# The first gate/up pair of an FFN: from a classical product to three seven-product units whose first two products run ahead

## The chip, the cores and the metric

The kernel runs on one core of one Trainium2 chip. The metric is the device time of one execution in microseconds (us), lower is better. It is called "same" below when the two kernels differ by less than 0.2%, which is about 4 us here.

PE is TensorE's matrix multiplication and PEld its weight load, DVE is VectorE, ACT is ScalarE, POOL is GpSimd, SP is the engine that issues most DMAs.

## What is computed

A decoder trunk of two layers over 512 tokens of width 1024, everything in float32. Each layer has two feed-forward blocks (FFNs), a mixer and a cross-attention, each behind an RMS norm, so there are four FFNs in the program:

```python
def swiglu_ffn(h, w_gu, w_down):
    gu = h @ w_gu                                  # 1024 -> 2 x 2816
    gate, up = jnp.split(gu, 2, axis=-1)
    return (jax.nn.silu(gate) * up) @ w_down       # 2816 -> 1024
...
x = x + 0.5 * rms_norm(swiglu_ffn(rms_norm(x, g_pre), w_gu, w_down), g_post)
```

## The kernel before

Every float32 product is made of three matmuls on rounded parts. `split` (L73) writes the rounded part `hi` of a tensor with a ScalarE copy (a cast, L74) and the remainder `lo` with a VectorE subtraction (L75); `mm3` (L77 to L81) then issues hi*hi, hi*lo and lo*hi into one PSUM bank. Weights are split in the same way after their DMA (`whi`, `wlo` in the profile).

**The norm in front of an FFN.** The 512 tokens are four tiles of 128. For each, `rms_transpose` (L160) takes the mean square (ACT L166, DVE L168 and L171), the reciprocal root on GpSimd (L158), and the scaled copy on ACT (L175). Its inner function `turn` transposes that tile on PE (L182, eight 128x128 blocks), multiplies by the gain on VectorE (L184) into the raw quarters, and splits the result. The first two tiles are turned before the FFN starts, the third and fourth inside it.

**An FFN** (`ffn`, L557) has 22 blocks of 128 hidden units, taken as 11 gate/up pairs `j` = 0, 2, ... 20 in three parts (0 to 8, 8 to 16, 16 to 22). Behind each of the first two parts comes the down-projection `seven_tm` (L336), whose matmuls are 128x512; behind the last comes `tm_last`.

**Ten of the pairs** go through `seven` (L292): a 2x2 block product by seven multiplications in place of eight. Its operands are the four quarters of the normalised activations (a11 and a12 are the first token half, a21 and a22 the second), and four combinations of them, x1 to x4, that `Quarters.ready` (L137) makes once for each FFN, after the fourth tile is turned. Each product is 24 matmuls of 128x256, so a pair has 7 x 24 = 168. Products p1 and p2 use a11 and a12, the first token half alone. The five others use x2, x1, x3, x4 and a22, and need all four tiles. Two weight sums, t1 and t3, are made by a DMA that adds on landing, issued on GpSimd's queue (L297, L302).

**The first pair, j = 0,** goes through `fm_quad` (L276), the classical product: four blocks of 24 matmuls over the first token half, then four over the second, 192 in all. `TURNS` puts the turns of tile 3 and tile 4 behind the first and the third block of the first half in the code 

```python
for c0 in (0, HALF):
    for i, (w, p_) in enumerate(zip(ws, ps)):
        fm_mm(p_, w, a, KD, c0, c0 + HALF)
        if c0 == 0 and i in TURNS:
            pre.turn()
```

Its weights are loaded and split early by `Prenorm.warm`. The order of each queue follows the code, a scheduler that moves instructions a little, and tile pools (PSUM pool `pa` for the banks `psa`, SBUF pool for `big`, `q4`, `raw`).

## Time and profile before

| | before |
|---|---|
| median of 3 runs | 2004.55 us (2003.13 to 2005.48) |
| the profiled execution | 2006.68 us, span 2005.0 us |
| PE busy | 1951.0 us, 97% of the span |
| DVE busy | 1488.6 us, 74% |
| ACT busy | 1038.3 us, 52% |
| POOL busy | 233.8 us, 12% |

The profiled execution is 2.1 us longer than the median; its span lacks 1.7 us of its own time. In rows of a timeline the first number is the start in us of the span, then the busy time, engine, line, operation, out<-in, shape and the number of instructions. What stands in brackets is the engine's idle time before it and what ended it. Matmuls of one row overlap; the time that one costs is the distance between starts.

### The profile page before, as it was taken

Reading aid. Unit: us, or ns where it says so; the run is one execution under the profiler, and the core shown is the slowest. Engines: PE = TensorE matmul, PEld = TensorE weight load, DVE = VectorE, ACT = ScalarE, POOL = GpSimd, SP = SyncE. Lnnn points to the kernel's source line nnn. Section 1 sums busy time; section 2 is a strip of 40 time slices with the busy share of each in tenths; the row PEclk is TensorE's granted clock in tenths of the full one; section 3 lists DMA queues with packets and bytes.
Section 4 is the critical chain, followed back from the end, with each engine's and each line's share of the span. In section 5 each row is a group of like instructions: output and inputs, shape, how many; then the busy total and the mean of one; then the engine's idle time right before and its main releaser. Section 6 shows DMA issues by size and latency. Waiting matters only on the chain.

```text
span 2005.0 us, 31807 instructions
## 1 busy us (share of the span) xinstructions
PE 1951.0 (97%) x12841; PEld 1784.3 (89%) x12841; DVE 1488.6 (74%) x1831; ACT 1038.3 (52%) x1477; POOL 233.8 (12%) x229
## 2 busy tenths in 40 slices
PE   7999999998998999999999999999999999999998
PEld 7989899887878889899898989999878889999897
DVE  6787877799956458877877887787666648776974
ACT  6555555543555455545555555555545545555552
POOL 1111110122001011111101111110000001111100
PEclk9999999999999999999999999999999999999999
DMA  7887884323642145887972788886152225898871
GB/s 201 219 213 185 204 207 140 118 85 126 224 154 95 53 107 142 208 204 187 221 213 65 172 217 179 202 212 185 63 179 74 85 53 138 209 211 200 202 187 42
DMA packets 250281, 319.90 MB, mean 160 GB/s; under 512 B 9756, under 2 KB 189556, under 8 KB 249110
## 3 DMA queue, kind: packets, MB, share of 16 engines
q1 hardware_dynamic: 193510, 242.32, 38.3%
q0 software_dynamic: 56448, 75.51, 21.9%
q8 instruction: 100, 1.64, 0.3%
q14 instruction: 47, 0.39, 0.1%
q10 hardware_dynamic: 176, 0.05, 0.0%
HBM read 311.54 MB, written 6.29 MB: 159 GB/s over the span
## 4 chain that ended last, share of the span: by engine, by line
PE 80%; DVE 8%; issue 5%; ACT 3%; POOL 2%; DMA 1%; POOLq 0%; ACTq 0%; SPq 0%; DVEq 0%
PE psa L81 26%; PE psa L80 26%; PE psa L79 26%; DVE wlo L75 2%; POOL r L158 1%; DVE big L75 1%; DVE big L730 1%; ACT q L175 1%; ACT whi L74 1%; PE tps L182 1%; DMA raw<-in_ffn_w_gu_dram 1%; ACT q L166 1%; DVE h L479 0%; DVE raw L404 0%; DVE q L394 0%
## 5 line engine op out<-in xcount | busy, mean ns | idle before, releaser
L81 PE MATMUL psa<-big,wlo 128*128 128x256 f32 (+1 forms) x3056 | 885.2, 290 | 6.6 <-DVE wlo L75 6.6
L79 PE MATMUL psa<-big,whi 128*128 128x256 f32 (+1 forms) x3056 | 884.4, 291 | 6.5 <-ACT big L74 4.6
L80 PE MATMUL psa<-big,whi 128*128 128x256 f32 (+1 forms) x3056 | 887.1, 291 | 0.8 <-DVE big L75 0.8
L74 ACT CAST whi<-raw 128x1024 fp32r<-128x1024 f32 x522 | 546.2, 1050 | 601.5 <-PE psa L80 263.1
L75 DVE TENSOR_TENSOR wlo<-raw,whi 128x1024 fp32r<-128x1024 f32 x522 | 636.0, 1225 | 252.8 <-ACT whi L74 250.1
L79 PEld LDWEIGHTS psa<-big,whi 128*128 128x128 f32 x3056 | 586.8, 193 | 17.1 <-ACT big L74 8.5
L81 PEld LDWEIGHTS psa<-big,wlo 128*128 128x128 f32 x3056 | 587.6, 193 | 15.0 <-DVE wlo L75 7.8
L80 PEld LDWEIGHTS psa<-big,whi 128*128 128x128 f32 x3056 | 588.3, 193 | 9.2 <-DVE big L75 1.8
L79 PE MATMUL psa<-whi,big 128*128 128x512 f32 x864 | 339.3, 393 | 7.7 <-ACT big L74 6.2
L80 PE MATMUL psa<-wlo,big 128*128 128x512 f32 x864 | 336.9, 390 | 0.0
L81 PE MATMUL psa<-whi,big 128*128 128x512 f32 x864 | 336.1, 392 | 0.4
L79 PEld LDWEIGHTS psa<-whi,big 128*128 128x128 f32 x864 | 162.4, 188 | 44.3 <-ACT big L74 10.3
L81 PEld LDWEIGHTS psa<-whi,big 128*128 128x128 f32 x864 | 162.2, 188 | 39.3 <-DVE big L75 5.8
L80 PEld LDWEIGHTS psa<-wlo,big 128*128 128x128 f32 x864 | 162.3, 188 | 33.1 <-DVE wlo L75 0.6
L302 POOL DMA_DIRECT2D raw<-in_ffn_w_gu_dram x40 | 51.6, 1289 | 582.1 <-DMA raw<-in_ffn_w_gu_dram 360.0
L158 POOL TENSOR_TENSOR r<-m,nhalf 128x1 f32<-128x1 f32 x74 | 49.0, 662 | 463.5 <-DVE m L533 181.7
L297 POOL DMA_DIRECT2D raw<-in_ffn_w_gu_dram x40 | 52.6, 1316 | 314.2 <-DMA raw<-in_ffn_w_gu_dram 236.3
L352 POOL DMA_DIRECT2D raw<-in_ffn_w_down_dram x48 | 57.4, 1227 | 261.9 <-DMA raw<-in_ffn_w_down_dram 187.0
L730 DVE SCALAR_TENSOR_TENSOR big<-big,par 128x511 f32<-128x511 f32 (+29 forms) x120 | 85.7, 770 | 0.0
L79 PE MATMUL psa<-big 128*128 128x512 f32 (+1 forms) x224 | 80.9, 363 | 0.8 <-ACT big L74 0.8
L80 PE MATMUL psa<-big 128*128 128x512 f32 (+1 forms) x224 | 80.7, 360 | 0.0
L81 PE MATMUL psa<-big 128*128 128x512 f32 (+1 forms) x224 | 80.2, 359 | 0.0
(150 smaller groups left out, 1658.6 us busy)
## 6 DMA issues: line engine op xcount, KB each, us to landing
raw<-in_ffn_w_gu_dram SPq DMA_DIRECT2D x216, 512.0 KB, 4.7
raw<-in_ffn_w_down_dram SPq DMA_DIRECT2D x120, 512.0 KB, 4.2
raw<-in_ffn_w_gu_dram POOLq DMA_DIRECT2D x80, 512.0 KB, 7.9
raw<-in_ffn_w_down_dram POOLq DMA_DIRECT2D x48, 512.0 KB, 7.8
raw<-in_xa_w_kv_dram SPq DMA_DIRECT2D x32, 512.0 KB, 3.5
raw<-in_ev_w_in_dram SPq DMA_DIRECT2D x16, 512.0 KB, 4.3
raw<-in_xa_w_q_dram SPq DMA_DIRECT2D x16, 512.0 KB, 4.4
raw<-in_xa_w_o_dram SPq DMA_DIRECT2D x16, 512.0 KB, 3.5
```

Source lines behind the costliest of these rows:

```text
L74: nc.scalar.copy(out=hi, in_=src)
L75: nc.vector.tensor_tensor(out=lo, in0=src, in1=hi.bitcast(F32), op=ALU.subtract)
L79: nc.tensor.matmul(out=ps, lhsT=lhs[0], rhs=rhs[0], start=start, stop=skip, skip_group_check=skip)
L80: nc.tensor.matmul(out=ps, lhsT=lhs[0], rhs=rhs[1], start=False, stop=skip, skip_group_check=skip)
L81: nc.tensor.matmul(out=ps, lhsT=lhs[1], rhs=rhs[0], start=False, stop=stop or skip, skip_group_check=skip)
L158: nc.gpsimd.tensor_tensor(out=r, in0=m, in1=nhalf.broadcast_to([P, n]), op=ALU.pow)
L166: nc.scalar.activation(out=xn[:, hs[i]], in_=src[:, hs[i]], func=AF.Square, accum_out=ss[i])
L175: nc.scalar.activation(out=xn[:, hs[i]], in_=src[:, hs[i]], func=AF.Copy, scale=r)
L297: nc.gpsimd.dma_start(out=t1, in_=fm_rows(w, 0, ca), accum_op=ALU.add)
L302: nc.gpsimd.dma_start(out=t3, in_=fm_rows(w, 1, cb), accum_op=ALU.add)
L352: nc.gpsimd.dma_start(out=raws[kk], in_=rows(kh, kk, ch), accum_op=ALU.add)
L730: nc.vector.scalar_tensor_tensor(out=acc[:, c, s_:], in0=z[:, c, :SEQ - s_], scalar=par[:, c, CONV - 1 - s_:CONV - s_], in1=acc[:, c, s_:] ...
```

## The change

The classical pair goes. All 11 pairs of an FFN run through `seven`, which becomes a generator that stops behind p1 and p2. The first three pairs (`AHEAD` = 3) do their p1 and p2 one after the other, with the turn of tile 3 behind the first unit's and that of tile 4 behind the second's; then each is run to its end. The first two units' p1 and p2 weights are the ones that `warm` prepares (columns 0 and 256 of the gate half in place of gate and up). `ready` works in place and makes x2 first, then x1, x3 and x4; the split of a21, which the classical pair alone used, is dropped.

```diff
+AHEAD = 3
...
+        def operand(src):
+            o = ops4()
+            split(o[:, 0], o[:, 1], src)
+            return o
...
             def block(self, i, c0, c1):
+                if c0 >= HALF and i == 0:
+                    return None
...
             def ready(self):
                 r0, r1 = self.raws
                 a11, a12, a21, a22 = r0[:, :, :HALF], r1[:, :, :HALF], r0[:, :, HALF:], r1[:, :, HALF:]
-                sub, add = ALU.subtract, ALU.add
-                xs = [ops4() for _ in range(4)]
-                e = qt([P, 4, HALF])
-                for i, (p_, q_, op) in enumerate(((a21, a22, sub), (e, a11, sub), (a12, e, add), (a11, a21, sub))):
-                    if i == 3:
-                        e = qt([P, 4, HALF])
-                    nc.vector.tensor_tensor(out=e, in0=p_, in1=q_, op=op)
-                    split(xs[i][:, 0], xs[i][:, 1], e)
-                self.x1, self.x2, self.x4, self.x3 = xs
+                sub = ALU.subtract
+                tt = nc.vector.tensor_tensor
+                tt(out=a11, in0=a11, in1=a21, op=sub)
+                tt(out=a21, in0=a21, in1=a22, op=sub)
+                nc.vector.scalar_tensor_tensor(out=a22, in0=a11, scalar=-1.0, in1=a22, op0=ALU.mult, op1=sub)
+                self.x2, self.x1, self.x3 = operand(a22), operand(a21), operand(a11)
+                tt(out=a12, in0=a12, in1=a22, op=ALU.add)
+                self.x4 = operand(a12)
...
-                    hi, lo = x.block(i, c0, c1)
-                    split(hi, lo, raw)
+                    to = x.block(i, c0, c1)
+                    if to:
+                        split(*to, raw)
...
-        def seven(w, ca, cb, x, done, mid=None):
-            t1 = fm_raw(w, 0, cb)
-            nc.gpsimd.dma_start(out=t1, in_=fm_rows(w, 0, ca), accum_op=ALU.add)
-            b11 = fm_raw(w, 0, ca)
-            b21 = fm_raw(w, 1, ca)
-            b22 = fm_raw(w, 1, cb)
-            t3 = fm_raw(w, 0, cb)
-            nc.gpsimd.dma_start(out=t3, in_=fm_rows(w, 1, cb), accum_op=ALU.add)
-            banks = {n: psa().rearrange("p (u n) -> p u n", u=2) for n in "ABC"}
+        def seven(w, ca, cb, x, done, mid=None, ahead=None):
+            later = ahead is not None
+            def sum_t1():
+                t1 = fm_raw(w, 0, cb)
+                nc.gpsimd.dma_start(out=t1, in_=fm_rows(w, 0, ca), accum_op=ALU.add)
+                return t1
+            if not later:
+                t1 = sum_t1()
+            b11, b21 = (None, None) if ahead else [fm_raw(w, i, ca) for i in range(2)]
+            def rest():
+                b22 = fm_raw(w, 1, cb)
+                t3 = fm_raw(w, 0, cb)
+                nc.gpsimd.dma_start(out=t3, in_=fm_rows(w, 1, cb), accum_op=ALU.add)
+                return b22, t3
+            if not later:
+                b22, t3 = rest()
+            banks = {n: psa().rearrange("p (u n) -> p u n", u=2) for n in "AB"}
             out_a = qt([P, 2, SEQ])
-            out_b = qt([P, 2, SEQ])
...
-            p1 = product("A", b11, x.a11, True)
+            wh = ahead or (None, None)
+            p1 = product("A", b11, x.at(0, 0), True, wh[0])
             nc.scalar.copy(out=out_a[:, :, lo_h], in_=p1)
-            p2 = product("B", b21, x.a12, True)
+            p2 = product("B", b21, x.at(0, 1), True, wh[1])
             nc.vector.tensor_tensor(out=out_a[:, :, lo_h], in0=p2, in1=out_a[:, :, lo_h], op=add)
+            yield
+            if later:
+                t1 = sum_t1()
+                b22, t3 = rest()
+                b11 = raw_tile([P, 4, 256])
+                b21 = fm_raw(w, 1, ca)
+            out_b = qt([P, 2, SEQ])
+            banks["C"] = psa().rearrange("p (u n) -> p u n", u=2)
...
                 for j in range(j0, j1, 2):
                     to = None if ending else r[(j - j0) // 4][:, (j - j0) % 4:(j - j0) % 4 + 2, :]
-                    if j == 0:
-                        ws = pre.ws
-                        ps = fm_quad([ws[0], ws[2], ws[1], ws[3]], pre, True)
...
-                        continue
...
-                    seven(w_gu, j * P, FF + j * P, pre.x, done, mid)
-                    if not ending and j - j0 == 2:
-                        a11 = ops4()
-                        split(a11[:, 0], a11[:, 1], r[0][:, :, :HALF])
+                    ahead = ([*pre.ws, ()][j // 2]) if j // 2 < AHEAD else None
+                    unit = seven(w_gu, j * P, FF + j * P, pre.x, done, mid, ahead)
+                    next(unit)
+                    if j // 2 < AHEAD:
+                        units.append(unit)
+                        if j // 2 < AHEAD - 1:
+                            pre.turn()
+                            continue
+                        for unit in units[:-1]:
+                            list(unit)
+                            prepare()
+                        unit = units[-1]
+                    list(unit)
+                    prepare()
...
-            return Prenorm(col(n, l), w[l], (0, FF), True)
+            return Prenorm(col(n, l), w[l], (0, 256), True)
```

PE's queue in the second FFN, before: the fourth tile's transposes (`tps`) stand in the fourth block of the first half (`psa_7156` is a bank of the classical pair, `psa_7418` to `psa_7420` those of pair 2; `big_7264` is x2, `big_7263` is x1).

```order
L81 MATMUL psa_7156<-big_7051,wlo_7120 128x256
...
L182 MATMUL tps_7255<-ident_85,q4_7138 128x128 x4
L79 MATMUL psa_7156<-big_7060,whi_7123 128x256
...
L79 MATMUL psa_7155<-big_7187,whi_7107 128x256
...
L79 MATMUL psa_7418<-big_7051,whi_7423 128x256
...
L79 MATMUL psa_7419<-big_7060,whi_7452 128x256
...
L79 MATMUL psa_7418<-big_7264,whi_7482 128x256
```

There are 156 matmuls between the second group of transposes and the first that reads x2. And now (`psa_7310`, `psa_7311` are the third unit's banks, `psa_7155` the first unit's, `big_7293` is x2, `big_7296` is x1):

```order
L184 MATMUL tps_7276<-ident_85,q4_7140 128x128 x4
L184 MATMUL tps_7282<-ident_85,q4_7140 128x128 x4
L80 MATMUL psa_7310<-big_7053,whi_7313 128x256
...
L82 MATMUL psa_7311<-big_7062,wlo_7343 128x256
L80 MATMUL psa_7155<-big_7293,whi_7385 128x256
L80 MATMUL psa_7383<-big_7296,whi_7414 128x256
L81 MATMUL psa_7155<-big_7293,whi_7385 128x256
```

48 matmuls are left between them, the third unit's p1 and p2, and one matmul of x1's product stands inside the first of x2's.

VectorE's queue at the same place, from the fourth tile's multiplies to x2's remainder, before:

```order
L184 TENSOR_TENSOR big_6720<-tps_7247,cols_101 128x4x128
L184 TENSOR_TENSOR big_6721<-tps_7255,cols_101 128x4x128
L75 TENSOR_TENSOR big_7187<-big_6720,big_7187 128x4x128
L146 TENSOR_TENSOR q4_7267<-big_6720,big_6721 128x1024
L75 TENSOR_TENSOR big_7196<-big_6721,big_7196 128x4x128
L146 TENSOR_TENSOR q4_7277<-big_6720 128x1024
L75 TENSOR_TENSOR big_7263<-q4_7267,big_7263 128x1024
L146 TENSOR_TENSOR q4_7267<-q4_7267,big_6720 128x1024
L75 TENSOR_TENSOR big_7264<-q4_7267,big_7264 128x1024
```

And now, with the three instructions that stand ahead of the multiplies:

```order
L76 TENSOR_TENSOR wlo_7343<-raw_7308,whi_7342 128x1024
L351 TENSOR_TENSOR raw_7379<-raw_7371,raw_7374 128x1024
L342 TENSOR_TENSOR q4_7225<-psa_7224,q4_7225 128x2x256
L186 TENSOR_TENSOR big_6722<-tps_7276,cols_101 128x4x128
L186 TENSOR_TENSOR big_6723<-tps_7282,cols_101 128x4x128
L145 TENSOR_TENSOR big_6722<-big_6722 128x4x256
L76 TENSOR_TENSOR big_7220<-big_6723,big_7220 128x4x128
L146 TENSOR_TENSOR big_6722<-big_6722,big_6723 128x4x256
L76 TENSOR_TENSOR wlo_7386<-raw_7379,whi_7385 128x1024
L147 SCALAR_TENSOR_TENSOR big_6723<-big_6722,big_6723 128x4x256
L342 TENSOR_TENSOR q4_7312<-psa_7311,q4_7312 128x2x256
L149 TENSOR_TENSOR big_6723<-big_6723 128x4x256
```

Behind the last row comes x2's remainder (L76). A weight remainder, a weight sum and an output sum now stand ahead of the multiplies, and a weight remainder and an output sum among the steps that lead to x2.

GpSimd's queue in the third FFN, before (`r1_10518` and `r1_10530` are square roots of the third tile's norms):

```order
L158 TENSOR_TENSOR r1_10518<-m_10515,nhalf_90 128x1
L297 DMA raw_11118<-in_ffn1_w_gu_dram 128x4x256
L158 TENSOR_TENSOR r1_10530<-m_10528,nhalf_90 128x1
```

And now:

```order
L160 TENSOR_TENSOR r1_10522<-m_10519,nhalf_90 128x1
L160 TENSOR_TENSOR r1_10534<-m_10532,nhalf_90 128x1
```

The accumulating DMA no longer stands between the two.

## Rows read from the trace of the kernel before

**Rows 1.** The page: busy time, share of the span and instructions of each engine:

```profile
PE 1951.0 (97%) x12841; PEld 1784.3 (89%) x12841; DVE 1488.6 (74%) x1831; ACT 1038.3 (52%) x1477; POOL 233.8 (12%) x229
```

**Rows 2.** The page: shares, by engine, of the chain that ended last:

```profile
PE 80%; DVE 8%; issue 5%; ACT 3%; POOL 2%; DMA 1%; POOLq 0%; ACTq 0%; SPq 0%; DVEq 0%
```

**Rows 3.** Timeline of PE: first 128x512 product of each FFN (start, us busy, engine, line):

```profile
104.08 0.40 PE L79 MATMUL psa<-whi,big 128*128 128x512 f32 x1
...
825.79 0.40 PE L79 MATMUL psa<-whi,big 128*128 128x512 f32 x1
...
1167.82 0.40 PE L79 MATMUL psa<-whi,big 128*128 128x512 f32 x1
...
1743.08 0.40 PE L79 MATMUL psa<-whi,big 128*128 128x512 f32 x1
```

**Rows 4.** Timeline of PE: gate/up matmuls, first and second FFN:

```profile
17.57 0.42 PE L81 MATMUL psa<-big,wlo 128*128 128x256 f32 x1
...
21.63 0.34 PE L80 MATMUL psa<-big,whi 128*128 128x256 f32 x1
...
752.02 0.28 PE L79 MATMUL psa<-big,whi 128*128 128x256 f32 x1
752.14 0.28 PE L80 MATMUL psa<-big,whi 128*128 128x256 f32 x1
```

**Rows 5.** Timeline of PE: tile-4 transposes of the second to fourth FFN, tile 3's of the third:

```profile
750.56 0.66 PE L182 MATMUL tps<-ident,q 128*128 128x128 f32 x4 [1.89 <-ACT q L175]
...
1082.93 0.66 PE L182 MATMUL tps<-ident,q 128*128 128x128 f32 x4
...
1091.92 1.27 PE L182 MATMUL tps<-ident,q 128*128 128x128 f32 x8 [0.17 <-ACT q L175]
...
1667.85 0.66 PE L182 MATMUL tps<-ident,q 128*128 128x128 f32 x4 [2.33 <-ACT q L175]
```

**Rows 6.** Timeline of DVE, second FFN: before the tile-4 multiplies, and from them:

```profile
748.87 0.16 DVE L171 SCALAR_TENSOR_TENSOR m<-ss,m 128x1 f32<-128x1 f32 x1
751.25 1.30 DVE L184 TENSOR_TENSOR big<-tps,cols 128x512 f32<-128x512 f32 x2 [2.23 <-PE tps L182]
...
753.24 1.22 DVE L146 TENSOR_TENSOR q<-big 128x1024 f32<-128x1024 f32 x1
754.38 0.68 DVE L75 TENSOR_TENSOR big<-big 128x512 fp32r<-128x512 f32 x1
754.98 1.22 DVE L146 TENSOR_TENSOR q<-big 128x1024 f32<-128x1024 f32 x1
```

**Rows 7.** Timeline of ACT, second FFN: the last norm output; a table load for Silu:

```profile
749.78 1.33 ACT L175 ACTIVATE q<-h,r 128x512 f32<-128x512 f32 x2 [0.95 <-POOL r L158]
...
755.56 1.28 ACT L571 ACT_TABLE_LOAD   x1
```

**Rows 8.** Timeline of POOL, second and third FFN: accumulating DMAs and square roots:

```profile
744.71 1.32 POOL L302 DMA_DIRECT2D raw<-in_ffn_w_gu_dram  x1 [7.94 <-ACT big L74]
745.55 1.08 POOL L158 TENSOR_TENSOR r<-m,nhalf 128x1 f32<-128x1 f32 x1
...
1080.22 1.31 POOL L297 DMA_DIRECT2D raw<-in_ffn_w_gu_dram  x1 [5.14 <-DVE m L171]
1081.04 1.08 POOL L158 TENSOR_TENSOR r<-m,nhalf 128x1 f32<-128x1 f32 x1
```

**Rows 9.** Timeline of PE: a long wait elsewhere in the program:

```profile
458.66 0.58 PE L81 MATMUL psa<-big,wlo 128*128 128x256 f32 x1 [2.76 <-DVE wlo L75]
```

**Rows 10.** Windows (range, length, PE, PEld, DVE, ACT, POOL, PEclk, DMA share, GB/s):

```profile
460.00:464.00 4.00, 4.00 (x28) 4.00 (x28) 4.00 (x7) 1.03 (x1) 0.00 (x0) 0.74 0.35 124
...
752.00:756.00 4.00, 4.00 (x34) 3.90 (x33) 3.93 (x5) 2.70 (x4) 0.00 (x0) 1.00 0.63 101
...
736.00:832.00 96.00, 92.39 (x738) 89.91 (x736) 76.40 (x84) 52.95 (x68) 11.84 (x11) 1.00 0.66 168
```

**Rows 11.** The page: accumulating DMAs of the gate/up weights, us to landing:

```profile
raw<-in_ffn_w_gu_dram POOLq DMA_DIRECT2D x80, 512.0 KB, 7.9
```

33 lines of the change are left out of this document (15 added, 18 removed).

## The prediction

> **What bounds the kernel now.** I read the page first. PE is busy for 97% of the span [rows 1], and the chain that ended last runs on PE for 80% of the span [rows 2], so time is won by fewer matmuls and lost by any wait of PE. VectorE at 74% is the next engine, busy enough to be late in a burst. Then I read PE's timeline at the four FFN entries, since only these four places change. At the low clock a 128x256 matmul costs 4.06 / 19 = 0.213 us (19 matmuls between the first two rows), at the high one 0.12 [rows 4]. The four marks that I compare are the starts of the first 128x512 product, that of the first down-projection: 104.08, 825.79, 1167.82 and 1743.08 [rows 3]. Up to the mark the program changes; behind it the queues are as before.
>
> **The change, part by part.**
>
> *Removed:* the classical pair has 192 matmuls and the seven-product one 168. That is 24 less for each FFN, or 24 x 0.12 = 2.9 us, and 11.5 us over four. This lies on PE and counts in full as long as PE does not wait.
>
> *Added beside the matmuls:* 24 more VectorE and 16 more ScalarE instructions, and 24 more weight DMAs (12.6 MB of 320 MB). Over the second FFN's first part ScalarE is busy 53 of 96 us and the DMA engines have a share of 0.66 [rows 10], so I cost these at nothing there. VectorE with 76 of 96 us has less room; what it has to do at the entry is the next part. If its cover went, each of its 24 instructions would cost at most 1.14 us (below), 27 us in all; I take nothing except where I count them one by one.
>
> *Moved:* this is where the gain goes. `ready` can start only when tile 4 is transposed, and PE then needs matmuls that do not use x2. Before, 156 of them stand there, 18.7 us. Now 48, the third unit's p1 and p2: 48 x 0.12 = 5.8 us. Against it stands VectorE's queue from the first multiply of tile 4 to x2's remainder, as the new order has it: two multiplies and two short instructions (a22's remainder and an output sum) at 0.60, from 754.38 to 754.98, and six long ones at 1.14, from 753.24 to 754.38 [rows 6]: the three in-place sums, the `scalar_tensor_tensor` among them, that the trace of before does not show (I take it as a two-input sum of the same size; between 0.60 and 2 x 1.14 it could be 0.5 less or 1.1 more), a weight remainder, the sum for x4 and x2's remainder. Together 4 x 0.60 + 6 x 1.14 = 9.2, say 9.3 us with the hand-over between engines. So PE waits even if VectorE starts at once: transposes start, first multiply 0.69 later [rows 5, 6], 9.3 more, less 1.15 for the transposes and 5.8 for the cover: 3.0 us. That the third unit's sums also stand ahead of the first multiply makes it longer:
>
> - Second FFN. The fourth tile's scaled norm starts at 749.78 and PE takes it up at 750.56 after 1.89 idle [rows 5, 7]. The copy of an output sum and its neighbours now stand ahead on ScalarE, so I start the transposes 0.55 later, at 751.1, and end them at 752.3. VectorE is through with the last mean at 749.0 [rows 6], has a weight remainder and a weight sum (1.14 each) and two output sums (0.6) in front, so it comes to the multiply at 752.6, 1.5 after the transposes began. x2 is ready at 752.6 + 9.3 = 761.9. PE's cover ends at 752.3 + 5.8 = 758.1: a wait of 3.9 us, cut by two lone matmuls that need only the rounded parts of x2 and x1. From x2 to the mark there are 526 matmuls, 63.1 us.
> - The clock. After a wait of 2.76 us [rows 9] the granted clock is 0.74 of full in the window behind it, while after the 1.89 us at 750.56 it is 1.00 [rows 5, 10]. Our wait is nearer to the first, so I charge some 20 matmuls at the low cadence, 20 x (0.213 - 0.12) = 1.9 us; the bounds are nothing and twice that.
> - So the mark comes at 761.9 + 63.1 + 1.9 = 826.9: **+1.1** against 825.79. The fourth FFN has the same distance from transposes to mark before (75.23 us in both, [rows 3, 5]): **+1.1** too.
> - Third FFN. Now the accumulating DMA (1.31 us) does not stand between tile 3's square roots on GpSimd [rows 8], so tile 3's transposes start about 1.3 earlier than 1082.93 [rows 5], at 1081.6. With 1.1 for them and 95 matmuls (11.4) tile 4's start at 1094.1; before, at 1091.92, since fewer matmuls stood ahead. First multiply 1.5 later as above, x2 at 1104.9, mark at 1169.9: **+2.1** against 1167.82.
> - First FFN. At 21.63, when the clock rises [rows 4], 22 of the 96 matmuls of the first two units are done; 74 x 0.12 and 1.1 for tile 3's transposes set tile 4's to 31.6. A Silu table load of 1.28 [rows 7] now stands on ScalarE ahead of tile 3's last cast, on which VectorE's next remainder waits, so the first multiply is 2.8 later, at 34.4; x2 at 43.7, mark at 108.7: **+4.6** against 104.08.
>
> Sum: 4.6 + 1.1 + 2.1 + 1.1 = +8.9 us. The profiled execution (2006.68) lies 2.1 above the median of the runs, 2004.55; the differences carry over, so I predict 2004.55 + 8.9 = **2013.5**.
>
> **The rivals.**
>
> *The clock holds.* If the wait costs no clock, 1.9 goes at each entry. In the second and fourth FFN the next wait then shows: the weight remainder of x1's product stands in VectorE's queue behind the other operands' remainders, four of 1.14 = 4.6 us behind x2's, against 2.9 us of x2's own matmuls, so 1.7 come back. The sum is 2.7 + 0.9 + 0.2 + 0.9 = +4.7, 2009.2. For it: the waits of 1.89 and 2.33 us at tile 4 of before [rows 5], the first followed by a clock of 1.00 [rows 10]. Against it: PE does hardly anything for 4 us. The Trainium skill, "TensorE: Matmul & The Clock Gate", section "Why this matters for your kernels", advises to leave no long idle gaps between bursts of matmuls, or the engine falls back; as the two lone matmuls cut the gap in pieces, the rule would speak for this rival. The wait in rows 9 agrees with the rule; no row of before shows a cut gap.
>
> *Late weight sums.* Units 2 and 3 each need t1 and t3, two accumulating DMAs for each 120 matmuls (14.4 us) where before it was two for each 168 (20.2 us), and they are issued only when the first unit has begun to finish. Each takes 7.9 us to land [rows 11] behind a load of the same tile. If they come 1 us late for each of the two units, each entry costs 2 us more: +16.9, 2021.5. For it: GpSimd is idle much of the time, but its DMA waits for what was loaded. Against it: the DMA share of 0.66 [rows 10] leaves room.
>
> *The stall is small (the other side).* If VectorE meets the first multiply as the transposes land, in place of 1.5 to 2.8 us later, and the clock holds, x2 comes 0.69 + 9.3 after the transposes. The price of the wait then is 3.0 us against 2.9 saved. GpSimd decides it: before, the square root of the last tile stood behind an accumulating DMA of 1.32 [rows 8], which now is issued later, so that the last tile can be normalised and transposed earlier and VectorE has its other work behind it. With the transposes at 750.2 in the second FFN x2 is ready at 760.2 and the mark at 823.3, -2.5, likewise in the fourth; third 1094.1 + 10.0 + 63.1 = 1167.2, -0.6; first 31.6 + 10.0 + 63.1 = 104.7, +0.6. Sum -5.0, 1999.5. The point from which it decides is the first multiply of tile 4 starting within 0.7 us of the first transpose. Against it: the new order puts a weight remainder and a weight sum in front of the multiply on the same engine, 2.3 us of work.
>
> That the change does not do what it says can be left out: the new order shows 168 matmuls and 48 of cover.
>
> **How the numbers follow.** Forecast 0.5; clock holds 0.2; late sums 0.15; small stall 0.1; 0.05 for anything beyond. About 0.2% (4 us) is what a measurement can tell from no change, so "same" reaches from 2000.5 to 2008.6. The clock's rival lies at its edge and takes half of its chance there, and the forecast's lower part a tenth: same 0.18. Small stall and a little more: faster 0.09. The rest is slower: 0.73. The range leaves out the small stall and what lies beyond late sums: 2003 to 2022, which also takes in the clock's double price (4 x 1.9 = 7.6 more than 2013.5).
>
> **What would show it.** In the profile of the changed kernel: 96 matmuls of 128x256 less; at each entry PE's idle of 3 to 5 us in front of the first matmuls with x2, put down to VectorE's `big` (its remainder) or ScalarE's cast; a granted clock below 1 in the 4 us behind it; VectorE's first multiply of tile 4 at least 1.5 us behind the first transpose; the marks 1 to 5 us later. It is wrong if the clock stays at 1.00 behind the wait, if the wait is under 2 us, or if PE waits for a DMA (`raw`) or a weight remainder in the units that finish.

## The result and the profile after

The changed kernel takes 2023.47 us (median of 4 runs, 2022.49 to 2025.78) where the kernel before takes 2005.01 on the same chip: a ratio of 1.0093, with a 95% interval of 1.0081 to 1.0106. That is slower, as forecast, but by 18.5 us and not by 8.9; it lies above the range of 2003 to 2022. The profiled executions differ by 15.8 us in their spans (2005.0 and 2020.8); the one of before lies 1.7 above its median, the one of after 1.0 below, which makes the 18.5.

The page of after, to be read against [rows 1, 2]:

```profile
PE 1949.8 (96%) x12745; PEld 1781.1 (88%) x12745; DVE 1512.2 (75%) x1855; ACT 1050.0 (52%) x1493; POOL 245.6 (12%) x237
...
PE 75%; DVE 10%; issue 5%; ACT 4%; POOL 2%; DMA 2%; POOLq 0%; ACTq 0%; SPq 0%; DVEq 0%
```

The 96 matmuls are gone, yet PE is busy 1.2 us less only (a matmul at the low clock, below, is busy 0.41 us in place of 0.28), and PE's share of the chain fell from 80% to 75%: 2 points went to VectorE, one each to ScalarE and the DMAs. The four marks (timeline of PE, first 128x512 product of each FFN, as in [rows 3]):

```profile
109.81 0.40 PE L80 MATMUL psa<-whi,big 128*128 128x512 f32 x1
...
834.96 0.40 PE L80 MATMUL psa<-whi,big 128*128 128x512 f32 x1
...
1178.27 0.40 PE L80 MATMUL psa<-whi,big 128*128 128x512 f32 x1
...
1758.87 0.40 PE L80 MATMUL psa<-whi,big 128*128 128x512 f32 x1
```

From here on an *entry* is the stretch from an earlier first 128x512 product to the FFN's mark (from 536.25, 1046.27 and 1388.30 in the trace of before, from 540.73, 1055.44 and 1398.74 in that of after; for the first, from the start of the span). The entries took 104.08, 289.54, 121.55 and 354.78 us and take 109.81, 294.23, 122.83 and 360.13. That is **+5.73, +4.69, +1.28 and +5.35**, 17.05 together; everything else is 1.2 shorter. PE's timeline at the second and the fourth entry (tile 4's transposes, then its waits up to the mark), to be read against [rows 5]:

```profile
757.85 1.27 PE L184 MATMUL tps<-ident,q 128*128 128x128 f32 x8 [2.37 <-ACT q L177]
...
767.07 0.39 PE L80 MATMUL psa<-big,whi 128*128 128x256 f32 x1 [2.20 <-ACT big L75]
...
768.02 0.38 PE L80 MATMUL psa<-big,whi 128*128 128x256 f32 x1 [0.56 <-ACT big L75]
...
768.86 0.38 PE L81 MATMUL psa<-big,whi 128*128 128x256 f32 x1 [0.47 <-DVE big L76]
...
773.96 0.39 PE L80 MATMUL psa<-big,whi 128*128 128x256 f32 x1 [0.52 <-ACT q L353]
...
791.66 0.39 PE L80 MATMUL psa<-big,whi 128*128 128x256 f32 x1 [0.40 <-ACT q L353]
...
1680.65 1.66 PE L184 MATMUL tps<-ident,q 128*128 128x128 f32 x8 [2.32 <-ACT q L177]
...
1691.17 0.38 PE L80 MATMUL psa<-big,whi 128*128 128x256 f32 x1 [1.96 <-ACT big L75]
...
1692.49 0.51 PE L81 MATMUL psa<-big,whi 128*128 128x256 f32 x1
...
1715.57 0.38 PE L80 MATMUL psa<-big,whi 128*128 128x256 f32 x1 [0.97 <-ACT q L353]
```

The wait for x2 comes in three pieces, its cast, x1's cast and x2's remainder, as the new order had it (3.23 us in all in the second entry). The last two rows of the second entry, and the last of the fourth with one of 0.61 at 1697.30, are waits for ScalarE's copies of output sums (L353) out of the banks. The granted clock behind the waits (windows, columns as in [rows 10]):

```profile
44.00:46.00 2.00, 1.90 (x9) 1.90 (x10) 2.00 (x3) 1.63 (x3) 1.28 (x1) 0.50 0.00 0
48.00:50.00 2.00, 2.00 (x12) 2.00 (x12) 2.00 (x3) 0.53 (x1) 0.00 (x0) 0.55 1.16 189
...
770.00:772.00 2.00, 2.00 (x12) 2.00 (x11) 2.00 (x2) 0.39 (x1) 0.00 (x0) 0.51 0.00 0
772.00:774.00 2.00, 1.48 (x8) 1.19 (x7) 2.00 (x3) 0.58 (x1) 0.00 (x0) 0.64 0.00 0
...
1682.00:1686.00 4.00, 4.00 (x25) 4.00 (x24) 3.22 (x5) 3.55 (x5) 0.00 (x0) 0.65 1.01 185
...
1692.00:1694.00 2.00, 1.89 (x8) 1.86 (x9) 2.00 (x3) 2.00 (x4) 0.00 (x0) 0.50 0.00 0
```

0.50 is the low level, 1.2 GHz. Behind x2's wait the clock is at it for some 3 us in the second to fourth entry and twice that in the first, and in the fourth once more, behind the wait in front of the transposes. At these places of the kernel before it stays at 1.00. VectorE's timeline from the first multiply of tile 4 to x2's remainder (second entry), the chain that the prediction added up:

```profile
758.54 1.31 DVE L186 TENSOR_TENSOR big<-tps,cols 128x512 f32<-128x512 f32 x2 [0.18 <-PE tps L184]
759.76 1.22 DVE L145 TENSOR_TENSOR big<-big 128x1024 f32<-128x1024 f32 x1
761.84 0.69 DVE L76 TENSOR_TENSOR big<-big 128x512 fp32r<-128x512 f32 x1 [0.86 <-ACT big L75]
...
764.72 1.22 DVE L147 SCALAR_TENSOR_TENSOR big<-big 128x1024 f32<-128x1024 f32 x1
...
767.59 4.63 DVE L76 TENSOR_TENSOR big<-big 128x1024 fp32r<-128x1024 f32 x4
```

L147 ends the doubt about the `scalar_tensor_tensor`: 1.14 to the next start, a sum like the others. The 0.86 in front of a22's remainder is new; ScalarE's timeline says why:

```profile
758.43 1.28 ACT L601 ACT_TABLE_LOAD   x1
759.72 0.63 ACT L601 ACTIVATE q<-q 128x512 f32<-128x512 f32 x1
760.26 1.04 ACT L75 CAST whi<-raw 128x1024 fp32r<-128x1024 f32 x1
761.19 0.61 ACT L75 CAST big<-big 128x512 fp32r<-128x512 f32 x1
```

a22's cast stands behind a table load for Silu, the Silu and a weight cast. In the fourth entry this takes 0.47, and VectorE also waits for PE, which runs tile 4's transposes and the third unit's products partly at the low clock (0.65 above, 1682 to 1686):

```profile
1682.35 0.69 DVE L186 TENSOR_TENSOR big<-tps,cols 128x512 f32<-128x512 f32 x1 [0.31 <-PE tps L184]
...
1684.64 0.69 DVE L76 TENSOR_TENSOR big<-big 128x512 fp32r<-128x512 f32 x1 [0.47 <-ACT big L75]
...
1689.31 0.69 DVE L342 TENSOR_TENSOR q<-psa,q 128x512 f32<-128x512 f32 x1 [0.57 <-PE psa L82]
```

And GpSimd's timeline of the second entry, to be read against [rows 8]:

```profile
723.18 1.37 POOL L310 DMA_DIRECT2D raw<-in_ffn_w_gu_dram  x1 [94.60 <-DMA raw<-in_ffn_w_gu_dram]
724.04 1.11 POOL L160 TENSOR_TENSOR r<-m,nhalf 128x1 f32<-128x1 f32 x1
...
750.75 1.33 POOL L320 DMA_DIRECT2D raw<-in_ffn_w_gu_dram  x1 [8.74 <-ACT whi L75]
751.60 1.06 POOL L160 TENSOR_TENSOR r<-m,nhalf 128x1 f32<-128x1 f32 x1
755.64 1.40 POOL L160 TENSOR_TENSOR r<-m,nhalf 128x1 f32<-128x1 f32 x1 [2.97 <-DVE m L173]
```

In the trace of before, the first DMA, the first tile's root and the last root:

```profile
707.70 1.37 POOL L297 DMA_DIRECT2D raw<-in_ffn_w_gu_dram  x1 [83.57 <-DMA raw<-in_ffn_w_gu_dram]
719.34 0.56 POOL L158 TENSOR_TENSOR r<-m,nhalf 128x1 f32<-128x1 f32 x1 [10.27 <-DVE m L475]
...
749.18 0.57 POOL L158 TENSOR_TENSOR r<-m,nhalf 128x1 f32<-128x1 f32 x1 [1.29 <-DVE m L171]
```

Now two accumulating DMAs stand directly in front of square roots, and the last root, on which tile 4's scaled copy waits, takes 1.40 where it took 0.57 before (749.18 in the trace of before). Why that costs 2.8 us is worked out below.

### The profile page after: what moved, and what is told of

It reads as the page before. It is cut to its first block, busy times and chain, and to the rows that moved or that the text cites. A ratio compares the mean times of both kernels' runs of the same rounds, so it can differ in the third digit from the quotient of the medians.

```text
span 2020.8 us, 31758 instructions
## 1 busy us (share of the span) xinstructions
PE 1949.8 (96%) x12745; PEld 1781.1 (88%) x12745; DVE 1512.2 (75%) x1855; ACT 1050.0 (52%) x1493; POOL 245.6 (12%) x237
## 4 chain that ended last, share of the span: by engine, by line
PE 75%; DVE 10%; issue 5%; ACT 4%; POOL 2%; DMA 2%; POOLq 0%; ACTq 0%; SPq 0%; DVEq 0%
PE psa L82 25%; PE psa L81 25%; PE psa L80 25%; DVE wlo L76 3%; DMA raw<-in_ffn_w_gu_dram 2%; DVE big L76 2%; POOL r L160 1%; ACT whi L75 1%; DVE big L762 1%; ACT q L177 1%; PE tps L184 1%; ACT q L168 1%; DVE q L419 0%; DVE raw L429 0%; DVE h L561 0%
## 5 line engine op out<-in xcount | busy, mean ns | idle before, releaser
L75 ACT CAST whi<-raw 128x1024 fp32r<-128x1024 f32 x534 | 559.2, 1050 | 623.6 <-PE psa L81 297.7
L76 DVE TENSOR_TENSOR wlo<-raw,whi 128x1024 fp32r<-128x1024 f32 x534 | 650.9, 1225 | 259.8 <-ACT whi L75 256.7
L80 PEld LDWEIGHTS psa<-big,whi 128*128 128x128 f32 x3024 | 585.4, 194 | 32.5 <-ACT big L75 21.3
L80 PEld LDWEIGHTS psa<-whi,big 128*128 128x128 f32 x864 | 162.4, 188 | 44.2 <-ACT big L75 10.3
L320 POOL DMA_DIRECT2D raw<-in_ffn_w_gu_dram x44 | 57.0, 1297 | 526.2 <-DMA raw<-in_ffn_w_gu_dram 305.5
L310 POOL DMA_DIRECT2D raw<-in_ffn_w_gu_dram x44 | 57.0, 1294 | 384.6 <-DMA raw<-in_ffn_w_gu_dram 245.7
L76 DVE TENSOR_TENSOR big<-big 128x1024 fp32r<-128x1024 f32 (+1 forms) x78 | 79.1, 1031 | 12.2 <-ACT big L75 12.2
L80 PE MATMUL psa<-big 128*128 128x512 f32 (+1 forms) x224 | 81.0, 363 | 0.8 <-ACT big L75 0.8
L81 PE MATMUL psa<-big 128*128 128x512 f32 (+1 forms) x224 | 80.8, 361 | 0.0
```

Source lines behind the costliest of these rows:

```text
L75: nc.scalar.copy(out=hi, in_=src)
L76: nc.vector.tensor_tensor(out=lo, in0=src, in1=hi.bitcast(F32), op=ALU.subtract)
L80: nc.tensor.matmul(out=ps, lhsT=lhs[0], rhs=rhs[0], start=start, stop=skip, skip_group_check=skip)
L81: nc.tensor.matmul(out=ps, lhsT=lhs[0], rhs=rhs[1], start=False, stop=skip, skip_group_check=skip)
L310: nc.gpsimd.dma_start(out=t1, in_=fm_rows(w, 0, ca), accum_op=ALU.add)
L320: nc.gpsimd.dma_start(out=t3, in_=fm_rows(w, 1, cb), accum_op=ALU.add)
```

## The experiments

Theory 1: PE's wait for x2, and what it does to the clock, is all that makes the change slow; its VectorE, ScalarE and GpSimd parts show where it comes from. Rivals: the new `ready` itself, weight sums that come late, or a limit of VectorE's whole work. Increments are those of the four entries against the trace of before, in us; intervals are for the ratio to before.

**The new `ready` alone.** The kernel before, with nothing changed but the in-place sums in the new order.

> The kernel before with one part of the change alone: the new way to make x1 to x4 (in place, x2 first). Its 156 matmuls of cover stay. Theory 1: nothing to see, within 0.2% of the kernel before (some 2005 on its chip). Rival (the in-place sums, which make VectorE wait for the casts that still read the quarters, cost time by themselves): 1 to 2 us at each entry, 2009 to 2013.

2006.02 us, ratio 1.0002 (0.9993 to 1.0012). The new sums cost nothing while 156 matmuls cover them.

**No wait for x2.** The first three units take a11 and a12 in place of x1 to x4 (so their products are not the real ones), and `ready` comes behind the third.

```diff
-            u2 = product("A", b11, x.x2, False)
+            z = x if not later else Early(x)
+            u2 = product("A", b11, z.x2, False)
```

> The changed kernel, but the first three units of each FFN multiply with a11 and a12 where x2, x1, x3 and x4 belong (so their five later products are not the real ones), and the sums for x1 to x4 are made behind the third unit. Nothing at the entry then waits for tile 4's chain on VectorE. Theory 1 (the loss is PE's wait for x2 and the low clock behind it): the four waits in the changed kernel's trace are 4.28, 3.23, 2.84 and 2.52 us, 12.9 in all, and the clock below 1 behind them costs some 7.5 (2.9, 1.5, 1.6, 1.5 from the granted clock of the windows), so 2023.5 - 20.4 = about 2003 us. Rival (the added weight loads, sums and VectorE work of the ahead units cost time by themselves, spread over the first part): above 2012, with new waits of PE on weight remainders or raw in the units that finish.

2000.02 us, 0.9973 (0.9956 to 0.9989; ten runs from 1994.42 to 2010.01). Increments -1.6, -1.6, -3.9 and -3.7, -10.8 together in its profiled execution, which is the fastest of the ten; by the medians the gain is 5.9. The 24 matmuls less at each entry are worth 11.5. So a saving is real, and the weight DMAs and the rest of the added work cost, by the medians, about half of it at most. What takes it back, and more, is what this run leaves out at the entry: the dependence on x1 to x4, and with it their sums and splits, which VectorE and ScalarE do later here. The run does not tell these two apart.

**Square roots ahead of the accumulating DMAs.** t1's DMA behind tile 1's root, t3's behind tile 4's.

```diff
-                nc.gpsimd.dma_start(out=t1, in_=fm_rows(w, 0, ca), accum_op=ALU.add)
+                with behind(0):
+                    nc.gpsimd.dma_start(out=t1, in_=fm_rows(w, 0, ca), accum_op=ALU.add)
```

> The changed kernel with GpSimd's queue put in another order: of the units that run ahead, t1's accumulating DMA is queued behind the first tile's square root of the norm and t3's behind the fourth tile's. In the changed kernel's trace a square root stands behind an accumulating DMA at 724.04 and 751.60 (and 1646.91, 1674.40) and comes 0.9 and 0.8 us later than without. Theory 1 (tile 4's arrival sets the entry of the second and fourth FFN): each of these entries comes 1.7 us earlier, 2023.5 - 3.4 = 2020.1, with the idle before tile 4's transposes down from 2.37 to about 0.7. Rival (VectorE's backlog of the ahead units would hold the multiply back anyway, as predicted): the transposes come earlier, the first multiply does not, 2023.5.

2016.91 us, 1.0054 (1.0039 to 1.0069): 6.6 less than the change. The 2.4 us in front of tile 4's transposes are gone in both entries. The fourth increment falls from +5.35 to +0.75, the second from +4.69 to +3.91 only, since the wait for x2 grows there, from 3.23 to 3.50 us, and the clock stays at its low level for twice as long behind it, 0.50 from 764 to 770 (timeline of PE, second entry):

```profile
754.51 0.66 PE L189 MATMUL tps<-ident,q 128*128 128x128 f32 x4
...
764.29 0.58 PE L80 MATMUL psa<-big,whi 128*128 128x256 f32 x1 [3.50 <-ACT big L75]
```

GpSimd's queue explains the part in front of the transposes, and a part of it lay beside VectorE's chain.

**Filling the wait.** 32 useless matmuls into a spare bank behind tile 4's transposes.

```diff
+                        fill = pst()
+                        for i in range(FILL):
+                            nc.tensor.matmul(out=fill[:, :HALF], lhsT=pre.x.at(0, 1)[:, 0, i % 4, :P],
+                                             rhs=pre.x.at(0, 0)[:, 0, i % 4], start=True, stop=True)
```

> The changed kernel with 32 matmuls of 128x256 behind the third unit's first two products, into a bank that nobody reads: 32 x 0.12 = 3.8 us of useless work where PE waits for x2 in the changed kernel (3.1 to 4.3 us). If the clock falls because of that wait and costs some 7.5 us in all, the fill gives this back less what it overshoots (about 1 us): 2016 to 2018, with a granted clock of 1.00 behind the first matmuls with x2. Rival (the clock falls for another reason, or costs nothing as in the rival of the prediction): 2023.5 or up to 2 more.

2027.75 us, 1.0112 (1.0086 to 1.0138), a miss. The clock stays at 1.00 behind the former wait, but now it falls earlier, behind the wait in front of tile 4's transposes (windows, second entry):

```profile
756.00:760.00 4.00, 3.90 (x20) 3.71 (x21) 3.13 (x5) 3.97 (x7) 0.57 (x1) 0.62 0.89 181
...
764.00:768.00 4.00, 4.00 (x36) 4.00 (x35) 3.41 (x5) 3.43 (x4) 0.00 (x0) 1.00 0.00 0
```

x2's wait is gone in the last three entries (in the first, pieces of 1.88, 0.56 and 0.46 us are left). But the fill itself costs 15.4 us (4 x 32 x 0.12), and PE runs into later waits for ScalarE's output copies, 1.58, 1.59 and 3.67 us in the second to fourth entry. So this run does not price the clock by itself; it shows that behind the first wait stands a second one.

**Both turns behind the first unit,** so that 96 matmuls cover x2 in place of 48.

```diff
-                        if j // 2 < AHEAD - 1:
+                        if j // 2 == 0:
+                            pre.turn()
                             pre.turn()
+                        if j // 2 < AHEAD - 1:
```

> The changed kernel with both turns, tile 3's and tile 4's, behind the first unit's two products, so that 96 matmuls stand between tile 4's transposes and x2. First and third FFN, where tile 4's norm is ready early: narrow theory: 96 matmuls cover the chain, the waits (4.28 and 2.84 us) and most of the low clock go, these entries 5 to 7 and 4 us shorter; wide theory: the queue of VectorE is as long as before, part of the wait stays, 2 to 3 us gained each. Second and fourth: PE now waits for tile 4 (some 13 us) ahead of 96 matmuls, and x2 comes no earlier: each about 2 to 4 us slower. Together 2017 to 2024, the entries apart tell.

2028.57 us, 1.0102 (1.0072 to 1.0132; one of the four runs 2017.71), a miss. The tile is not normalised earlier for it: PE waits 2.79 us for it in the second entry (now with fewer matmuls ahead), 1.97 for x2 all the same, and up to 4.17 at an output copy in the fourth.

**The operands in halves.** Tile 3's columns of x1 to x4 as soon as it is turned.

```diff
-                if self.turned == NT:
-                    self.x.ready()
+                if self.turned > 2:
+                    self.x.ready(self.turned - 3)
```

> The changed kernel with the sums and splits for x1 to x4 made in two halves: the columns of the third tile as soon as it is turned, those of the fourth behind the fourth. Behind tile 4's multiplies VectorE then has two multiplies, a22's remainder, three half sums, the half sum for x4, an output sum and x2's half remainder at 0.60 each and one weight remainder at 1.14: 6.5 us in place of 9.3. Theory 1 (the length of the chain on VectorE behind tile 4 sets the wait): 2.8 us less at each entry, 11 in all, and some of the low clock's 7.5, so 2005 to 2012. Rival (VectorE's total work at the entry sets it, not the chain): the extra half instructions and their fixed part make it the same or slower, 2023 to 2026.

2037.13 us, 1.0163 (1.0141 to 1.0184), a miss, and the worst with these buffers. Half the sums earlier are twice as many instructions, and they push the weights' parts back: 3.55 us on a weight remainder and 3.60 on a weight cast in the second entry, +13.7 there.

**x2 first on VectorE.** With the roots as above, x1, x3, x4 and the output sums are queued behind x2's remainder, each where its product needs it, and PE's products are kept whole, one behind the other.

```diff
-                self.x2, self.x1, self.x3 = operand(a22), operand(a21), operand(a11)
...
+                self.x2 = operand(e)
+                self.first = rest[0]
```

> The kernel with reordered square roots (2016.9 us) and three units ahead, with x2 taken out of the queue: its sum goes to a tile of its own, directly behind the first in-place sum, and the sums for x1 and x4 and the third unit's output sum are queued behind x2's remainder; the first unit's later products keep their order on PE. Work on VectorE is the same, PE's cover too (48 matmuls). Behind the first multiply stand two multiplies (1.2), one sum, a22's remainder (0.6), x2's sum, two weight remainders and x2's remainder (1.14 each): 7.5 us in place of 9.3 to 10.3. Theory 1 (what stands ahead of x2 in VectorE's queue sets the wait, and the clock follows the wait): 1.8 to 2.8 us less wait at each entry and about half of the low clock's 7.5, so 2016.9 - 8 - 4 = about 2005, at the level of the kernel before. Rival (total VectorE work, the wait moves to x1's product and stays as long): 2014 to 2018.

2012.05 us, 1.0037 (1.0022 to 1.0051): more than half way back. What is left are waits of 1.1 to 2.5 us for x2's cast, which stands on ScalarE behind a weight cast, and of 0.7 to 2.0 for the operands' remainders. What PE's new order alone gave, no run shows.

**And x2 first on ScalarE.** Weight casts and a22's own parts are held behind the casts of the operands.

```diff
-                wh = wh or parts(raw, (P, 4, 256))
+                hold = hold and later and x.first
+                with tc.issue_after(x.tops[-2]) if hold else nullcontext():
+                    wh = wh or parts(raw, (P, 4, 256))
```

> The kernel with x2 first (2012.05 us), and the same done for ScalarE: there x2's cast stood behind the cast of the weights of the first unit's fourth product, which waited for their accumulating DMA (2.68, 1.99 and 2.38 us at the second, fourth and third entry). Now each later weight cast is queued behind the cast of the operand before it, the remainder of tile 4's a22 behind x1's, and the weight sum for the unit's last product behind x1's remainder. Work is the same. x2's remainder ends 5.8 to 6.4 us behind the first multiply, PE's cover 6.2 behind it; x1's product then waits for the rest of VectorE's queue, some 1.2 us. Theory 1 (PE waits for whatever stands ahead of x2 in the in-order queues of VectorE and ScalarE; the clock falls only behind the long wait): waits of 1 to 1.5 us an entry in place of 2.7 to 4.2, and no low clock, so 2012 - 4 x 2 - 5 = about 1998 to 2002, below the kernel before. Rival (the entry lacks VectorE time whatever the order): 2010 to 2013.

2011.09 us, 1.0031 (1.0021 to 1.0042, 12 runs), the best of the real variants, and still slower than before; 1998 to 2002 was expected. PE's timeline of the second entry, in a profiled execution of 2014.75 us:

```profile
762.30 0.38 PE L85 MATMUL psa<-big,whi 128*128 128x256 f32 x1 [0.87 <-DVE big L80]
...
766.38 0.39 PE L85 MATMUL psa<-big,whi 128*128 128x256 f32 x1 [0.88 <-DVE big L80]
...
774.39 0.39 PE L85 MATMUL psa<-big,whi 128*128 128x256 f32 x1 [1.99 <-DVE big L80]
...
794.67 0.58 PE L84 MATMUL psa<-big,whi 128*128 128x256 f32 x1 [2.87 <-DVE q L397]
```

x2, x1 and x4 each come 0.9 to 2.0 us late, one behind the other, and VectorE has hardly a gap there (windows):

```profile
768.00:778.00 10.00, 8.01 (x67) 7.81 (x66) 9.16 (x10) 4.38 (x6) 1.30 (x1) 1.00 0.81 193
```

With 9.16 of 10 us busy, VectorE is near its limit here. But the waits for operands are much alike at all four entries, 3.1 to 4.2 us each, while the increments are +4.8, +5.4, +0.1 and -1.1. What the first two have besides is the low clock, for some 3 and 7 us, and the second the last row of PE above: a wait behind a weight sum, for which VectorE itself stands idle (timeline of VectorE; a window behind it):

```profile
789.19 1.22 DVE L391 TENSOR_TENSOR raw<-raw 128x1024 f32<-128x1024 f32 x1 [4.19 <-issue]
...
795.00:800.00 5.00, 5.00 (x25) 5.00 (x25) 4.39 (x5) 1.06 (x1) 0.00 (x0) 0.50 1.15 273
```

The sum's accumulating DMA was issued at 780.82 and landed at 789.11, by its semaphore in the trace.

**Less VectorE work.** As the last, without the remainders of x1, x3 and x4 (x2's stands in for them, so the products are not the real ones).

```diff
-                        self.made[n] = operand(self.src[n])
+                        o = ops4()
+                        top[:] = [nc.scalar.copy(out=o[:, 0], in_=self.src[n]).ins]
+                        self.made[n] = Mix(o, self.x2)
```

> The last kernel (2011.1 us) with three of VectorE's instructions less at each entry, none of which stands ahead of x2: the remainders of x1, x3 and x4 are left out, and x2's stands in their place (so the products with x1, x3 and x4 are not the real ones). That kernel's waits at an entry are 0.87 us for x2's remainder, 0.88 for x1's and 2.00 for x4's. If VectorE's time at the entry is what lacks (3 x 1.14 = 3.4 us less of it), the last two waits go, 2.9 us at each of four entries: 2011 - 11.5 = about 1999 to 2001. Rival (what is left is not VectorE: weight sums, the clock, the queue of the DMAs): 2008 to 2011.

2013.89 us, 1.0049 (1.0032 to 1.0066), a miss. The waits for x1 and x4 are gone and the second entry is 0.7 us shorter than before. In the third and fourth another wait has come, of 4.5 us (timelines of PE, VectorE and GpSimd, fourth entry):

```profile
1710.77 0.58 PE L84 MATMUL psa<-big,whi 128*128 128x256 f32 x1 [4.45 <-DVE q L406]
...
1705.29 1.23 DVE L400 TENSOR_TENSOR raw<-raw 128x1024 f32<-128x1024 f32 x1 [4.47 <-issue]
...
1696.08 1.27 POOL L354 DMA_DIRECT2D raw<-in_ffn_w_gu_dram  x1 [7.39 <-DVE wlo L80]
```

The accumulating DMA waits 7.39 us until a weight remainder frees its tile, and is issued 9.2 before VectorE can take up the weight sum that needs it; it landed at 1705.21, 0.08 ahead of the sum. These are the late weight sums, the second rival of the prediction; they show once x2 no longer hides them.

**The sums on GpSimd.** x4's sum and two of the remainders go there.

```diff
+        def pooled(src):
...
+            nc.gpsimd.tensor_tensor(out=o[:, 1], in0=src, in1=o[:, 0].bitcast(F32), op=ALU.subtract)
```

> The last kernel (2011.1 us) with real results and three of VectorE's instructions at each entry moved to GpSimd, which is idle there: the sum for x4 and the remainders of x3 and x4. What GpSimd needs for a 128x1024 two-input instruction no run shows yet. At up to 2.9 us each (one product of PE) x3's and x4's waits go and the entry is some 2 us shorter: about 2003. Rival: GpSimd and VectorE disturb each other (the square root of 0.55 us took 1.40 beside VectorE's two-input sums), x3 and x4 come later than now, and the accumulating DMAs queued behind them too: 2012 to 2030.

2030.14 us, 1.0125 (1.0107 to 1.0144). GpSimd's timeline, second entry:

```profile
763.27 2.37 POOL L155 TENSOR_TENSOR big<-big 128x1024 f32<-128x1024 f32 x1 [4.07 <-DVE big L176]
770.55 5.27 POOL L125 TENSOR_TENSOR big<-big 128x1024 fp32r<-128x1024 f32 x2 [4.92 <-ACT big L124]
```

A sum takes 2.37 and a remainder 2.6 us where VectorE takes 1.14, and the next accumulating DMA waits behind them.

**A fourth unit ahead** (96 matmuls of cover), its output sums in a weight tile, with the roots as above:

```diff
-AHEAD = 3
+AHEAD = 4
...
-            out_a = qt([P, 2, SEQ])
+            out_a = raw_tile([P, 2, SEQ]) if fourth else qt([P, 2, SEQ])
```

> The kernel of the run with reordered square roots (2016.9 us), and a fourth unit's first two products ahead too, behind the third's: PE's cover behind tile 4's transposes goes from 48 to 96 matmuls, 5.8 to 11.5 us. Theory 1, narrow (the wait is x2's chain of 9.3 us against PE's cover): the cover is now longer than the chain, the waits of some 4 us go at all four entries, with the low clock behind them: about 1998 to 2002. Theory 1, wide (VectorE's whole queue sets it, since the sums and remainders that belong to the weights of the fourth unit and of the first unit's third product stand in the same queue, the latter behind x1's, x3's and x4's remainders): the first triple of the third product has its weight remainder 15.5 us behind the first multiply, against some 12 us of PE's work, so a wait of 3 to 4 us stays, put down to DVE's wlo in place of big: 2010 to 2016.

2032.17 us, 1.0140 (1.0119 to 1.0162), a miss. The wait for x2 is gone, and in its place PE waits 3.9 to 5.4 us for the cast of the first weight sum. With VectorE's work in the order of need:

> The kernel with four units ahead and reordered square roots, and VectorE's queue in the order in which PE needs things: x2, the remainder of its weights, then x1 and the remainder of its weights, and so on (the sum and the splits of x1, x3 and x4 are queued behind the remainder of the weights of the product before). Work is the same as in the run with four ahead. Wide theory (the loss is what stands ahead of the next product in VectorE's queue): x2 is ready 8.1 and its weights 10.4 us behind the first multiply, inside 11.5 us of cover, and each later product (2.9 us of PE) needs 2.3 us of VectorE, so no wait over 0.7 us stays at an entry: the 24 matmuls saved at each FFN show in full, 2005 - 11.5 = about 1993 to 1998, faster than both kernels. Rival (the entry has too little VectorE time whatever the order): 2003 to 2012.

2032.69 us, 1.0134 (1.0117 to 1.0152), a miss: 3.06 for the weight sum, which stands on VectorE behind an output sum that waits for PE, and 2.7 to 5.1 later. What the fourth unit gives in cover it takes in weight tiles.

**More weight tiles.** 9 raw tiles in place of 7, paid for by one operand buffer (12 in place of 13): the kernel before as control, the change, the best variant, and that with four units.

```diff
-N_S = 13
+N_S = 12
...
-N_R = 7
+N_R = 9
```

> The kernel before with the same buffers, nine raw and twelve operand ones: the control. Both theories: as before within 0.2%, 2003 to 2007, unless one operand buffer less holds something up elsewhere.

> The changed kernel with nine raw weight buffers in place of seven, paid for by one operand buffer less (twelve in place of thirteen). Theory 1 (the wait for x2 sets the entries of the changed kernel; the late weight sums only come into play where that wait is shortened): the waits for x2 stay at 2.8 to 4.3 us, only the small later waits (0.4 to 1.0 us, put down to ScalarE's copies) may go: 2020 to 2024. Rival (late weight sums cost the changed kernel its time): 2010 or less.

> The kernel with x2 and the casts first (2011.1 us) with nine raw buffers. Theory 1 with the raw buffers as the next limit: in its trace and in that of the run with less VectorE work, VectorE stood up to 4.5 us at the weight sum of the second unit (t1 + b22), whose accumulating DMA is issued late since it has no raw buffer, and PE waited 1.7 to 4.5 us behind it. These waits go; those for x2, x1 and x4 (0.87, 0.88, 2.00) stay, since VectorE's work is the same: 2003 to 2008. Rival (the sums are late for another reason): 2010 to 2012.

> The last kernel with a fourth unit's two products ahead (its output sum queued behind x1's remainder, so that it holds nothing up): 96 matmuls, 11.5 us, of cover for 2.9 us more of VectorE work ahead of x4. Up to x4's remainder VectorE then needs some 22 us behind the first multiply, PE has 20.6 us of work up to there: waits of 1.4 us an entry at most in place of 3.75. The 24 matmuls saved at each FFN (11.5 us in all) then show for about half: 1996 to 2001, faster than both kernels by over 0.2%. Rival (the fourth unit's output and the sums lack buffers again, or tile 4 comes too late): 2005 to 2020.

2056.42, 2079.29, 2077.67 and 2081.46 us, none as expected. The control itself loses 52 us, mostly outside the entries (PE's waits for casts of operands rise from 11.6 to 34.6 us), so nothing is won by these sizes; against it the three are 22.9, 21.3 and 25.0 slower. With four units the wait for the weight sum falls from 3.06 to 0.76 us, but x4's remainder (2.0) and an output copy (3.1 to 4.2) still make PE wait. A pool with more weight tiles and all 13 operand buffers was not tried.

No variant that computes the real products beats the kernel before.

## Why the prediction was wrong in size

Direction, place and kind were right: 96 matmuls less, PE waiting at each entry for x2's cast and remainder, the clock below 1 behind it, nothing lost elsewhere. Split at the first transpose of tile 4, against before:

| entry | forecast: transposes, from there to the mark | measured |
|---|---|---|
| first | +3.2, +1.4 | +3.67, +2.06 |
| second | +0.55, +0.57 | **+2.81, +1.88** |
| third | +2.2, -0.1 | +2.09, -0.81 |
| fourth | +0.55, +0.57 | **+2.36, +2.99** |

First and third came within 1.2 us. Of the 9.6 us between forecast and result 7.8 lie in the second and fourth; the rest is small (the first and third 0.3 together, the medians 2.7 further apart than the profiled executions, the other stretches 1.2 shorter). The steps:

- **"So I start the transposes 0.55 later"** is the step that failed most, by 2.3 and 1.8 us. The 0.55 was ScalarE's copy; it cost 0.41. GpSimd's queue was not counted. The first tile's root now stands behind an accumulating DMA (723.18; before, it was issued at 707.70, 11.6 us ahead of the root): 0.76 and 0.83. The DMA in front of tile 4's first root, there before too [rows 8], is released later, by a weight cast in the second entry and an earlier load in the fourth: 0.81 and 0.30. The last root takes 1.40 for 0.57, 0.83 in the second entry and 0.82 in the fourth. 0.41 + 0.76 + 0.81 + 0.83 = 2.81, and 0.41 + 0.83 + 0.30 + 0.82 = 2.36. That GpSimd is idle 88% of the time had hidden it; taking the DMAs away from the roots took away the idle time in front of the transposes.
- **The chain of 9.3 us** was exact in the first (34.76 to 44.10) and third entry. In the second it took 10.3: 0.86 of it is a22's cast behind the table load, which I had costed in the first entry only. In the fourth it took 11.1: 0.47 for that cast, and 0.31 and 0.57 in which VectorE waited for PE, at the low clock since the idle time in front of the transposes; that a wait for tile 4 could cost clock too was not in the sum. Against it VectorE met the first multiply 0.69 after the transposes and not 1.5, since they came later: -0.8.
- **From x2 to the mark** I put 63.1 + 1.9 = 65.0; measured 66.1 and 66.4. What the sum did not have are two waits for output copies in each entry, 0.92 and 1.58 us. The first of each (0.52 and 0.61) is PE's own order: in the second and fourth FFN two matmuls of x3's product, which goes on in x2's bank (`psa_7155` in the second), stand directly behind x2's product, so they wait until the copy out of that bank is done. In the first and third FFN 23 matmuls of x1's product stand between, and there is no such wait. The second of each (0.40 and 0.97) has a copy that came late itself, behind VectorE: ScalarE waited 0.66 for its `big` (L602). That this lateness goes back to the four remainders in one piece (767.59, 4.63 us) is likely, but not shown.
- **The clock** was right in kind. 1.9 was charged for each entry. At the low level 1 - 0.12 / 0.213 = 0.44 of the time is lost; the windows show it for 6 us in the first entry (44 to 50), 3 in the second (770 to 773), 3 in the third (1115 to 1118) and twice 3 in the fourth (1682 to 1685, 1692 to 1695). That is 2.6, 1.3, 1.3 and 2.6 us, 7.8 where 7.6 were charged; that the sums agree is luck, since no entry cost 1.9. The rival that it holds is out. The Trainium skill, "TensorE: Matmul & The Clock Gate", section "Why this matters for your kernels", warns of idle gaps between bursts; I had read it so that two lone matmuls in the gap would help. The waits of 2.20, 0.56 and 0.47 ended at 0.51 (770 to 772): they did not. With 32 matmuls in the gap the clock stayed at 1.00 behind it in the second and third entry. So the trace agrees with the rule and not with my reading of it.
- **The small stall** had the first multiply right, 0.7 after the transposes in the second and fourth entry, but the transposes were late themselves: its premise that tile 4's roots would be free of the DMA was wrong. **Late weight sums** did not show as a wait for DMA; they were hidden behind x2, as the variants show.
- **The signs.** An idle of 3 to 5 us for x2 held in the first two entries (4.28 and 3.23; then 2.84 and 2.52), a first multiply at least 1.5 behind the transposes in the first alone (2.68; then 0.69, 1.04 and 0.70). The wait of 3.9 us for the second FFN is 3.8 by its own terms, 761.9 less 758.1; nothing else hangs on it.

What is shown: without x1 to x4 at the entry the change wins (2000.0); with them 23.5 us are lost against that, of which GpSimd's order is 6.6 (2016.9) and the order on VectorE, ScalarE and PE 5.8 (2011.1). Theory 1 does not hold as it stood: where x2's wait was taken away (the fill in three entries, the fourth unit in all), other waits took its place and the time did not fall. What is argued: that the remaining 11 (some 3 either way, by the interval of the first run) are mostly VectorE's total at the entry. The classical pair gave it 192 matmuls with four weight remainders; a seven-product unit has seven remainders, two weight sums and three output sums for 168. The run with fewer remainders agrees in part: its waits for x1 and x4 are gone and its second entry is shorter than before, but so was the fourth entry with all remainders, and weight tiles limit it next. Late weight sums and the low clock have a share in the 11 that no run separates, and no run had both limits lifted.

## What to carry over

A cheaper product that needs a derived operand moves its price from PE to the engine that makes the operand: count what that engine must finish, from the last input to the first use, against the matmuls that do not need it, before counting matmuls saved. Walk every queue that stands ahead of that last input, the idlest one too, and ask of each DMA on it when it is released. Read PE's own order as well: a matmul that was moved ahead into a bank still to be copied waits for the copy. When a wait is shortened, expect the next one within a few microseconds, and look at the whole load of the engine before reordering its queue.

## What was not expected of the hardware

A square root on GpSimd (128x1) took 0.55 to 0.57 us in 57 of its 74 cases in the trace of after. The one at 755.64 took 1.40, wholly beside two VectorE instructions with both inputs in SBUF:

```profile
755.41 1.22 DVE L76 TENSOR_TENSOR wlo<-raw,whi 128x1024 fp32r<-128x1024 f32 x1
756.55 1.22 DVE L351 TENSOR_TENSOR raw<-raw 128x1024 f32<-128x1024 f32 x1
```

The fourth entry's is the same, 1.40, and the longest is 3.20 (614.40). In the run with the roots first the same root took 0.86, beside a remainder of 0.69 and the start of one of 1.22. Spans on GpSimd are rough, but ScalarE's scaled copy, which waits for it, started at 757.07, 0.03 after that end. The Trainium skill, "GPSIMD Engine Reference", section "1. Specifications", says that GpSimd's SBUF interfaces are shared with VectorE and that VectorE's instructions with two SBUF inputs contend for them. The trace agrees, and has the price of one case; it was not measured by itself.

Equal idle times did not do the same to the clock. After 2.33 us in front of tile 4's transposes the granted clock was 1.00 in the kernel before (1667.85), after 2.32 at the same place it was 0.65 now (1680.65), and after 2.37 in the second entry 1.00. In the trace of the best variant a wait of 2.0 us for x4 is followed by the low clock in the first entry and not in the third and fourth. What else decides it no run here shows.
